# Which slot an expert's token takes: rank r in slot 7r modulo 104 instead of slot r

## The chip, the cores and the metric

One core of one Trainium2 chip runs the whole program. The metric is device time in microseconds; a comparison is made between runs of the kernel before and after on the same chip.

## The reference, cut to what matters

One decoder block over 1024 tokens of width 1024. The first two thirds (norm, projections, gated convolution, forgetting attention, merge, output projection) are not touched by the change. What matters is the mixture of experts behind it: every token chooses one group of 8 experts and in it its two best experts.

```python
lg = h @ w_rg + b_rg                     # 4 groups
g_idx = argmax(lg)
le_g = (h @ w_re + b_re) of group g_idx  # 8 experts
top_v, top_i = top_k(le_g, 2)
w_k = softmax(top_v) * p_sel
for e in range(32):
    a = silu(h @ w_gate[e]) * (h @ w_up[e])
    out = out + comb[..., e:e + 1] * (a @ w_down[e])
```

An expert's w_gate and w_up are 1024 x 256 each, its w_down 256 x 1024, all in float32: 3 MiB of weights an expert.

## The kernel before, in words

**Stages.** Activations and weights are split into a high and a low part (float32r), and a product is made of three matmuls. `start`, `attention` and `mid` come first; `out_proj` computes the residual sum, the second norm (written to the DRAM tensor `d_h2`, one row a token) and the routing, 256 tokens at a time; `moe` runs the 32 experts, in the order of `self.order` (one expert of each group in turn).

**Routing.** `route` finds each token's two experts and its rank in each of them: how many earlier tokens chose the same expert, counted with triangular matmuls. Then it builds, for 128 tokens and each of the two choices, a 0/1 matrix `lhs` with a row for each token and a column for each slot: `lhs[p, j]` is 1 where `slots[j]` equals the token's rank (L1053). `self.slots` is a constant row, filled by an iota on GpSimd in `route_consts` (L895, through the helper's L892). Matmuls of `lhs` with the token numbers and with the combine weights put them at (slot, expert) in the tables `tabi` and `tabw`. A slot that no token takes keeps the index 1024, which is out of bounds, and the weight 0. `route_index` and `scatter` write the same records to a table in DRAM, by rank, for the loop over overflow at the end (tokens of rank 104 and above, CAP = 104).

```python
for k, b in kb:
    eng = nc.vector if g == 3 else nc.gpsimd
    eng.tensor_scalar(lhs[:, b, k, :], self.slots, rk[:, b, k:k + 1], None, op0=ALU.is_equal)
```

**One expert.** `gather_rows` (L1370) fetches the expert's rows of `d_h2` into `xg`, 104 partitions x 4 KB, by an indirect DMA from GpSimd whose indices are the expert's column of `tabi`; a row whose index is out of bounds is left out. There are two `xg` buffers, so an expert's gather is issued as soon as the transposes of the expert two before have read theirs. `tokens` transposes the rows on TensorE (L1387) and splits them; `front` multiplies with gate and up (L1413, L1422 to L1424); `turned` transposes the activations; `back` multiplies with w_down (L1457 to L1459), scales on VectorE (L1460), and adds the 104 rows into the output with an indirect DMA that accumulates (L1461), with the same indices. An add waits for the fourth add before it.

**Order on TensorE.** `in_turn` fixes it: front of expert n up to its first piece, the turn of expert n - 1, the rest of the front, the transposes of expert n + 1, the back of expert n - 1.

**Weights.** They come in pieces of 512 KB (128 x 1024 float32), four for gate and up and two for down, or two pieces in one transfer of 1 MB. `plan_room` lays out the buffers: 34 pieces are loaded ahead (`raw_fill`, from L1183 on), and then a piece is loaded whenever one of the ring's 30 buffers becomes free (`piece_done`, `raw_next`; the transfers are issued at L1224 and L1249). All go through SP's queue, in order. ScalarE makes the high part of a piece (L1360) and VectorE the low part (L1361). Eight completion semaphores serve SP's transfers in turn, so a transfer is issued only when the eighth before it has landed.

Of the kernel before, what the change touches and what calls it, by code (L numbers as in the profile page):

```python
# [12 lines left out]
F32 = mybir.dt.float32  # L13
# [10 lines left out]
P = 128  # L24
# [64 lines left out]
class Builder:  # L89
# [797 lines left out]
    def route_consts(self, dp):  # L887
        nc = self.nc

        def iota(name, shape, pattern, base, mult):  # L890
            t = dp.tile(shape, F32, name=name, bufs=1)
            nc.gpsimd.iota(t, pattern=pattern, base=base, channel_multiplier=mult, allow_small_or_imprecise_dtypes=True)  # L892
            return t

        self.slots = iota("slots", [P, P], [[1, P]], 0, 0)  # L895
        self.val = dp.tile([P, TB, 2], F32, name="val", bufs=1)
        nc.gpsimd.iota(self.val[:, :, 0:1], pattern=[[0, TB], [0, 1]], base=P, channel_multiplier=-1,
                       allow_small_or_imprecise_dtypes=True)
        nc.gpsimd.iota(self.val[:, :, 1:2], pattern=[[-P, TB], [0, 1]], base=S - P, channel_multiplier=0,
                       allow_small_or_imprecise_dtypes=True)  # L900
        self.tacc = dp.tile([P, 2, NE], F32, name="tacc", bufs=1)
        nc.vector.memset(self.tacc[:, 0, :], float(S))
        nc.vector.memset(self.tacc[:, 1, :], 0.0)
        self.rev = dp.tile([P, NE], F32, name="rev", bufs=1)
        nc.gpsimd.iota(self.rev, pattern=[[-1, NE]], base=NE, channel_multiplier=0,
                       allow_small_or_imprecise_dtypes=True)
        self.tok = dp.tile([P, TB], I32, name="tok", bufs=1)
        nc.gpsimd.iota(self.tok, pattern=[[P, TB]], base=0, channel_multiplier=1)
        nc.vector.memset(self.csum, 0.0)
        ini = dp.tile([P, 96, 2], I32, name="ini", bufs=1)  # L910
        nc.gpsimd.iota(ini[:, :, 0:1].rearrange("p (a g e) o -> p a g (e o)", a=3, g=4),
                       pattern=[[0, 3], [P, 4], [0, 8]], base=S, channel_multiplier=1)
        nc.vector.memset(ini[:, :, 1:2], 0)
        self.tab_init = [nc.sync.dma_start(out=self.d_tab[:, q * 96:(q + 1) * 96, :], in_=ini) for q in range(3)]
        self.recs = []
# [615 lines left out]
```

## Time and profile before

| | us |
|---|---|
| median of three runs | 1213.91 (1209.13 to 1214.06) |
| the profiled execution | 1215.14 |
| its span, first to last instruction | 1213.4 |
| TensorE busy | 1124.9 |
| VectorE busy | 796.1 |
| ScalarE busy | 565.3 |
| GpSimd busy | 290.4 |

The span is that of one profiled execution; its own time is 1.2 us above the median of the runs. The experts run from about 850 us to the end. In the rows below PE is TensorE, PEld its weight loads, DVE VectorE, ACT ScalarE, POOL GpSimd, and SP the engine whose queue issues the weight transfers; a q behind an engine's name stands for its sequencer. "L1461" is a line of the kernel. An arrow with a name says what ended the wait.

### The profile page before, as it was taken

Reading aid. Unit: us, or ns where it says so; the run is one execution under the profiler, and the core shown is the slowest. Engines: PE = TensorE matmul, PEld = TensorE weight load, DVE = VectorE, ACT = ScalarE, POOL = GpSimd, SP = SyncE. Lnnn points to the kernel's source line nnn. Section 1 sums busy time; section 2 is a strip of 40 time slices with the busy share of each in tenths; the row PEclk is TensorE's granted clock in tenths of the full one; section 3 lists DMA queues with packets and bytes.
Section 4 is the critical chain, followed back from the end, with each engine's and each line's share of the span. In section 5 each row is a group of like instructions: output and inputs, shape, how many; then the busy total and the mean of one; then the engine's idle time right before and its main releaser. Section 6 shows DMA issues by size and latency. Waiting matters only on the chain. (4 is left out here: it accounts for less than half of the span.)

```text
span 1213.4 us, 15884 instructions
## 1 busy us (share of the span) xinstructions
PE 1124.9 (93%) x5489; PEld 894.9 (74%) x5489; DVE 796.1 (66%) x1527; ACT 565.3 (47%) x960; POOL 290.4 (24%) x280
## 2 busy tenths in 40 slices
PE   3799999999999989999999999996999997987984
PEld 3788888998898777788888888885666665655652
DVE  6855565565555665554666656787688887685863
ACT  6734544544543564323232222333666655564651
POOL 2030320330230120000000002545245434252431
PEclk8899999999999999999999999998999998998998
DMA  8514122112312424755665673347999989999961
GB/s 302 205 47 127 36 72 78 60 53 60 97 35 54 111 70 166 240 157 161 208 207 189 211 289 143 153 174 265 308 324 309 324 281 338 303 351 301 320 192 27
DMA packets 65427, 222.94 MB, mean 184 GB/s; under 512 B 11809, under 2 KB 16513, under 8 KB 56642
## 3 DMA queue, kind: packets, MB, share of 16 engines
q1 hardware_dynamic: 54370, 200.63, 49.3%
q0 software_dynamic: 9824, 17.09, 6.1%
q10 hardware_dynamic: 1152, 4.19, 0.9%
q8 instruction: 44, 0.72, 0.2%
q14 instruction: 37, 0.30, 0.1%
HBM read 201.57 MB, written 26.58 MB: 188 GB/s over the span
## 5 line engine op out<-in xcount | busy, mean ns | idle before, releaser
L1461 POOL DMA_INDIRECT out_dram<-y,tabi x32 | 85.5, 2672 | 152.6 <-DVE y L1460 133.3
L432 POOL TENSOR_SCALAR p<-p,su 128x128 f32<-128x128 f32 (+3 forms) x64 | 48.2, 759 | 234.2 <-DVE su L431 210.0
L101 ACT ACTIVATE wphi<-wpraw 128x1024 fp32r<-128x1024 f32 x42 | 44.6, 1063 | 122.9 <-DMA wpraw<-in_w_g_dram 53.2
L494 PE MATMUL gps<-hhi,wphi 128*128 128x512 f32 x256 | 101.6, 397 | 0.3 <-ACT wphi L101 0.3
L496 PE MATMUL gps<-hhi,wplo 128*128 128x512 f32 x256 | 101.3, 396 | 0.2 <-DVE wplo L102 0.2
L495 PE MATMUL gps<-hlo,wphi 128*128 128x512 f32 x256 | 101.2, 395 | 0.0
L446 DVE TENSOR_TENSOR pl<-pT,ph 128x512 fp32r<-128x512 f32 (+1 forms) x96 | 51.2, 552 | 46.7 <-ACT ph L445 46.3
L494 PE MATMUL cps<-hhi,wphi 128*128 128x512 f32 x192 | 77.1, 402 | 0.9 <-ACT v L325 0.6
L495 PE MATMUL cps<-hlo,wphi 128*128 128x512 f32 x192 | 76.3, 398 | 0.0
L188 DVE SCALAR_TENSOR_TENSOR adaw<-adaw,cb 128x1024 f32<-128x1024 f32 x32 | 39.2, 1225 | 55.2 <-DMA adaw<-in_w_ada_dram 55.2
L496 PE MATMUL cps<-hhi,wplo 128*128 128x512 f32 x192 | 74.9, 398 | 0.0
L445 ACT ACTIVATE ph<-pT 128x512 fp32r<-128x512 f32 (+1 forms) x96 | 44.4, 489 | 64.4 <-PE pT L442 58.8
L102 DVE TENSOR_TENSOR wplo<-wpraw,wphi 128x1024 fp32r<-128x1024 f32 x42 | 51.4, 1223 | 25.6 <-ACT wphi L101 25.6
L102 DVE TENSOR_TENSOR wplo<-waraw,wphi 128x768 fp32r<-128x768 f32 (+2 forms) x40 | 40.0, 1000 | 42.1 <-ACT wphi L101 41.2
L312 PE MATMUL qkvp<-wplo,hhi 128*128 128x384 f32 x192 | 65.8, 343 | 0.8 <-DVE wplo L102 0.8
L311 PE MATMUL qkvp<-wphi,hhi 128*128 128x384 f32 x192 | 65.5, 349 | 0.6 <-ACT wphi L101 0.6
L313 PE MATMUL qkvp<-wphi,hlo 128*128 128x384 f32 x192 | 65.2, 340 | 0.0
L1360 ACT ACTIVATE wphi<-H 128x1024 fp32r<-128x1024 f32 x39 | 41.1, 1060 | 40.7 <-DMA H<-in_w_gu_dram 18.3
L430 ACT ACTIVATE p<-p,m 128x128 f32<-128x128 f32 (+3 forms) x64 | 49.4, 774 | 22.8 <-DVE m L427 12.9
L1457 PE MATMUL yp<-wphi,ah 128*104 128x512 f32 x84 | 37.3, 444 | 22.1 <-DVE y L1460 14.6
L1370 POOL DMA_INDIRECT xg<-d_h,tabi x32 | 42.5, 1327 | 63.8 <-PE xT L1387 50.0
L494 PEld LDWEIGHTS gps<-hhi,wphi 128*128 128x128 f32 x256 | 48.1, 188 | 12.4 <-ACT wphi L101 0.8
(500 smaller groups left out, 3154.1 us busy)
## 6 DMA issues: line engine op xcount, KB each, us to landing
H<-in_w_gu_dram SPq DMA_DIRECT2D x24, 1024.0 KB
adaw<-in_w_ada_dram SPq DMA_DIRECT2D x32, 512.0 KB
wpraw<-in_w_g_dram SPq DMA_DIRECT2D x30, 512.0 KB
stage<-in_w_gu_dram SPq DMA_DIRECT2D x14, 1024.0 KB
wplo<-in_w_gu_dram SPq DMA_DIRECT2D x24, 512.0 KB
H<-in_w_d_dram SPq DMA_DIRECT2D x12, 1024.0 KB
wpraw<-in_w_d_dram SPq DMA_DIRECT2D x20, 512.0 KB
ld<-in_w_ada_dram SPq DMA_DIRECT2D x16, 512.0 KB
```

The source lines that it names most:

```text
L101: nc.scalar.activation(hi, raw, AF.Copy)
L102: (lo_eng or nc.vector).tensor_tensor(out=lo, in0=raw, in1=hi.bitcast(F32), op=ALU.subtract)
L311: nc.tensor.matmul(ps, hi[:, kc, sl], wh, start=(kc == 0), stop=False)
L312: nc.tensor.matmul(ps, hi[:, kc, sl], wl, start=False, stop=False)
L313: nc.tensor.matmul(ps, lo[:, kc, sl], wh, start=False, stop=(kc == KC - 1))
L430: nc.scalar.activation(pr, pr, AF.Exp, bias=m[:, b:b + 1], scale=-1.0, accum_out=su)
L432: nc.gpsimd.tensor_scalar(pr, pr, su, 1.0, op0=ALU.mult, op1=ALU.mult)
L446: nc.vector.tensor_tensor(out=pl[:, off:], in0=tp[:, off:], in1=ph[:, off:].bitcast(F32), op=ALU.subtract)
L494: nc.tensor.matmul(ps, wh, hi[:, kc, :], start=(kc == 0), stop=False)
L495: nc.tensor.matmul(ps, wh, lo[:, kc, :], start=False, stop=False)
L496: nc.tensor.matmul(ps, wl, hi[:, kc, :], start=False, stop=(kc == KC - 1))
L1461: ins = nc.gpsimd.indirect_dma_start(out=self.out, out_offset=bass.IndirectOffsetOnAxis(ap=idx, axis=0), in_=y, in_offset=None, bounds_che ...
```

## The change

The constant row `slots` holds another order of the same numbers 0 to 127. Before, slot j held j. Now slot 7a + b holds a + 15b, for a from 0 to 14 and b from 0 to 6, so that the token of rank r finds itself in slot 7r modulo 104 (ranks 0 to 103); slots 104 to 127 keep their own numbers. One iota becomes two.

```diff
-        self.slots = iota("slots", [P, P], [[1, P]], 0, 0)
+
+        self.slots = dp.tile([P, P], F32, name="slots", bufs=1)
+        nc.gpsimd.iota(self.slots[:, 0:105].rearrange("p (a b) -> p a b", b=7), pattern=[[1, 15], [15, 7]], base=0,
+                       channel_multiplier=0, allow_small_or_imprecise_dtypes=True)
+        nc.gpsimd.iota(self.slots[:, 105:P], pattern=[[1, P - 105]], base=105, channel_multiplier=0,
+                       allow_small_or_imprecise_dtypes=True)
         self.val = dp.tile([P, TB, 2], F32, name="val", bufs=1)
```

## Rows read from the trace of the kernel before

**Rows 1.** The page: the span, and busy time of each engine.

```profile
span 1213.4 us, 15884 instructions
...
PE 1124.9 (93%) x5489; PEld 894.9 (74%) x5489; DVE 796.1 (66%) x1527; ACT 565.3 (47%) x960; POOL 290.4 (24%) x280
```

**Rows 2.** Stretches: busy time of each engine, granted clock, DMA busy share, GB/s.

```profile
core 0: us, PE busy (x) PEld busy (x) DVE busy (x) ACT busy (x) POOL busy (x), PEclk, DMA share, GB/s
10.00:20.00 10.00, 5.61 (x29) 5.15 (x30) 8.85 (x35) 8.88 (x17) 2.82 (x4) 0.91 1.02 411
860.00:980.00 120.00, 118.09 (x540) 80.59 (x541) 103.50 (x112) 82.33 (x113) 56.15 (x36) 1.00 0.99 315
980.00:1180.00 200.00, 176.26 (x771) 119.67 (x769) 145.28 (x168) 110.11 (x152) 76.51 (x34) 0.94 0.91 302
```

**Rows 3.** Timeline of GpSimd, adds alone: start, length, operation, idle time before.

```profile
873.82 2.38 POOL L1461 DMA_INDIRECT out_dram<-y,tabi  x1 [0.58 <-DVE y L1460]
...
940.87 2.32 POOL L1461 DMA_INDIRECT out_dram<-y,tabi  x1 [3.46 <-DVE y L1460]
...
961.18 2.60 POOL L1461 DMA_INDIRECT out_dram<-y,tabi  x1 [4.59 <-DVE al L1443]
...
1187.94 2.32 POOL L1461 DMA_INDIRECT out_dram<-y,tabi  x1 [10.01 <-DVE y L1460]
1194.49 1.61 POOL L1461 DMA_INDIRECT out_dram<-y,tabi  x1 [4.24 <-DVE al L1443]
1198.91 1.61 POOL L1461 DMA_INDIRECT out_dram<-y,tabi  x1 [2.81 <-DVEq L1322]
```

**Rows 4.** Waits, 980 to 1200 us: waiting, released by, total us, times, longest.

```profile
ACT wphi L1360 <- DMA H<-in_w_gu_dram: 18.3, 4, 8.7
ACT row L1360 <- DMA stage<-in_w_gu_dram: 16.6, 2, 8.4
...
PE yp L1457 <- ACT xh L1389: 7.6, 1, 7.6
```

**Rows 5.** Waits of SP's queue, 860 to 1170 us, the four largest.

```profile
SPq L1249 <- DMA H<-in_w_gu_dram: 32.1, 9, 4.9
SPq L1224 <- DMA H<-in_w_gu_dram: 24.0, 7, 4.2
SPq L1224 <- DMA stage<-in_w_gu_dram: 22.4, 7, 4.4
SPq L1224 <- DMA wplo<-in_w_gu_dram: 21.7, 14, 3.4
```

**Rows 6.** The adds at 1187.94, 1194.49 and 1198.91 us, each alone: issue to landing.

```profile
DMA to landing us min/median/max: 6.9/6.9/6.9
...
DMA to landing us min/median/max: 6.1/6.1/6.1
...
DMA to landing us min/median/max: 6.0/6.0/6.0
```

**Rows 7.** The constant row's instructions: count, shortest, median, longest ns, first and last start.

```profile
L1053 POOL TENSOR_SCALAR tlhs<-slots,rk x12: 598/610/1582, 772.4 to 825.8; 128x128 bf16<-128x128 f32 x12
...
L892 POOL IOTA slots<- x1: 251/251/251, 696.2 to 696.2; 128x128 f32 x1
...
  DVE adaw L188: 227.2, 1
```

**Rows 8.** Stretch of the last add's transfers, columns as in rows 2.

```profile
1201.00:1204.50 3.50, 0.00 (x0) 0.00 (x0) 0.00 (x0) 0.00 (x0) 0.00 (x0) 0.73 0.37 53
```

**Rows 9.** Waits, 838 to 860 us, the largest of TensorE.

```profile
PE xT L1387 <- DMA xg<-d_h,tabi: 6.6, 1, 6.6
```

**Rows 10.** The page's groups of GpSimd's indirect DMAs: busy us, mean ns, idle before.

```profile
L1461 POOL DMA_INDIRECT out_dram<-y,tabi x32 | 85.5, 2672 | 152.6 <-DVE y L1460 133.3
...
L1370 POOL DMA_INDIRECT xg<-d_h,tabi x32 | 42.5, 1327 | 63.8 <-PE xT L1387 50.0
```

## The prediction

> **What bounds the kernel now.** I read the page first: TensorE is busy for 1124.9 of 1213.4 us, so time can only be won where it waits or runs slowly [rows 1]. The table of stretches shows where that is. From 860 to 980 us, in the expert stage, TensorE works 118.09 of 120 us at a granted clock of 1.00 (the 2.4 GHz level); from 980 to 1180 us it works 176.26 of 200 us, and the clock falls to 0.94 on average [rows 2]. The timeline of GpSimd gives the pace, because each expert ends in one scatter-add. The first to the eighth start at 873.82 and 940.87 us, seven periods of 9.58 us; that is TensorE's own pace. The tenth starts at 961.18 us, 1.1 us behind that pace, and the thirtieth at 1187.94 us: twenty periods of 11.34 us [rows 3]. At 9.58 us the thirtieth would start at 873.82 + 29 x 9.58 = 1151.6 us. So some 36.3 us of the expert stage are stalls. The waits say for what: ScalarE, which splits the weights, waits for weight transfers (18.3 and 16.6 us in its two largest rows), and TensorE's down products wait behind it [rows 4]. The weights' own queue, SP, does not issue ahead either: in its four largest rows alone it waits 100.2 of 310 us for an *earlier weight transfer to land* [rows 5]. A transfer has landed when the last of the 16 DMA engines is done with its part. The stage waits, then, for the slowest of them.
>
> **Why one engine may be slower than another.** In 10 to 20 us, with weights and tokens alone, the 16 engines moved 411 GB/s; from 860 to 980 us, with gathers and adds beside the weights, 315 GB/s, at the same full busy share [rows 2]. The reference's router, run on the inputs, gives 45 to 101 tokens an expert, 64 on average (2048 over 32), packed into slots 0 upwards; the other slots hold an index out of bounds and move no row. The last three adds hold 77, 63 and 45 rows, and land 6.9, 6.1 and 6.0 us after issue [rows 6]. 40% more rows take the same time: the number of rows does not set it, the fullest group does. This is what comes out if neighbouring slots go to the same engine in equal groups. I take 13 groups of 8 (104 in equal parts, at most 16); with groups of 7 the sums below shrink by an eighth and keep their sign.
>
> **The edit itself.** One iota of 0.251 us on GpSimd becomes two. Such iotas are next to free: GpSimd had been idle 227.2 us before it, at 696.2 us, and the first reader starts at 772.4 us [rows 7]. 76 us cover a second one of the same price; uncovered it would cost 0.25 us. The readers' compare has the same shape, every matmul, copy and DMA of the experts the same count and size, and the weights and indices go through the same 0/1 matrix, so they move with the rows. No expert has over 104 tokens, so the overflow loop runs zero times before and after. No wait is added.
>
> **What an engine carries, an expert.** Weights: 3 MiB over 16 engines are 48 pieces of 4 KB; at 411/16 = 25.7 GB/s a piece takes 0.159 us: 7.65 us. A gathered row is one such piece, 0.159 us. An added row has no row of its own among other traffic, so I bound it: not under a plain piece, 0.159 us; and in the tail, where nothing else runs, 0.37 of 16 engines x 3.5 us = 20.7 us for 45 rows, 0.46 us each, first-row latency included [rows 8]. If 11.34 us were all the work of a full engine, it would be (11.34 - 7.65 - 8 x 0.159)/8 = 0.30 us; that pace still had a lead to live on, so I take 0.38, between this and the tail.
> - Before, a group of 8 that is always full (slots 0 to 39 are, with 45 tokens or more): 7.65 + 8 x (0.159 + 0.38) = 11.96 us (10.2 to 12.6).
> - After, slot 7r mod 104 puts 64/13 = 4.92 rows in each group: 7.65 + 4.92 x 0.539 = 10.30 us (9.2 to 10.7).
>
> TensorE wants 9.58 us. So before, each expert loses 2.4 us of the lead that the buffers gave the weights; the first ten experts ran without stalls, so the lead is worth about 24 us. After, 31 experts lose 0.72 x 31 = 22 us: it just lasts. At the upper price they lose 1.11 x 31 = 34 us, 10 us of stall; at 0.30 us an add, none. I take 5 us.
>
> **The sum.** Stalls removed 36.3, stalls left 5: 31.3 us. The last add is on the path, since its landing ends the work: 45 rows fill groups of 8 now and of 4 after, so 4 x 0.44 us (8 rows in the 3.5 us of that window) = 1.8 us less; between 0 and 1.8, and I take it whole. The first gather holds TensorE for 6.6 us [rows 9]; three rows fewer on its fullest engine are 3 x 0.159 = 0.5 us, twice that with a weight piece between, and I count none. Together 33.1 us. The profiled execution took 1215.14 us, 1.2 above the median of 1213.91, so 1182.0 us against its own time is **1181 us** against the median. What is late next is TensorE itself, at 9.58 us an expert; its clock, lower only where it stalls, should stay at 1.00.
>
> **Rivals.**
> - *The rows are spread already.* If the group that starts a transfer moved from DMA to DMA, each engine would have 64/16 x 0.539 = 2.2 us of rows, 9.8 us in all, before the change as after. Then nothing changes: 1214 us. Against it: 9.8 us would use up 0.2 us of lead an expert and stall nowhere, while the stage falls back 36 us. For it: the tail shows groups, not which engine a group begins on. The Trainium skill speaks for this rival: its page "DMA: Bandwidth & Descriptors", section "Why a DMA increments its semaphore by 16 and not by 1", says that a GpSimd DMA whose outer size gives fewer than 16 engines takes consecutive ones from a round-robin cursor. By that rule the sum would be zero. 7%.
> - *A common limit.* If HBM, or whatever all engines share, sets the rate, moving rows between engines wins little. A third of the stalls might still go: 1202 to 1214 us. Against it stands 411 GB/s early on, against 302 to 315 in the stage [rows 2]; for it, the mean busy share of 0.99, which unequal engines should lower unless packets that share an engine are counted over each other. The same page, section "Bandwidth", says that for HBM to SBUF the HBM side binds at about 358 GB/s for a core; the 411 GB/s of this trace disagree. 8%.
> - *GpSimd becomes the bound, and it is slower.* Descriptors are made on GpSimd: 2672 + 1327 ns an expert, 4.0 of 9.58 us [rows 10]. Filled and empty slots now alternate. If that made the lists costlier, it decides from 2.4 times on (9.58 us), and makes the kernel slower from 2.8 times (11.34 us); at three times, 12.0 us, it costs some 30 x 0.66 = 20 us: 1234 us. Against it: the last add, of 45 rows, took 1.61 us, as did that of 63, and that of 77 took 2.32 [rows 3], no trend that nears a factor of 2. 3%.
>
> That the edit doesn't do what it says I rule out: the first iota writes a + 15b to slot 7a + b, and 7(a + 15b) = 7a + b modulo 104.
>
> **How the numbers follow.** My forecast has 82%. Its own bounds: no stall left, the last add and 1 us at the first gather give 1175 us; 10 us of stall and nothing at the end, 1188 us. Beyond that the lead may be worth less than I read, or part of the limit be common: up to a third of the gain left, 1203 us. The range is 1173 to 1203 us; the rest, about 2 in 10, lies with the rivals. A measurement of this kernel tells about 0.5%, 6 us, from no change. Faster: the forecast and half of the common limit, 86%. Same: the spread rows and three parts in eight of the common limit, 10%. Slower: GpSimd and what remains of it, 4%.
>
> **What would show it.** Right: adds 9.6 to 10 us apart throughout, SP's waits for landings far shorter, TensorE busy over 190 of 200 us in the stretch that was 176, more GB/s there, and the last adds' landings unequal, in the order of their rows, and shorter than 6 us. Wrong: an unchanged pace of 11.3 us, or last adds that still land in 6 us whatever their rows (then neighbours did not share an engine). If the landings shorten and the pace does not, the limit is common; if indirect DMAs on GpSimd grow past twice their time, it is the third rival.

## The result and the profile after

The kernel with the changed slots took **1195.86 us** (median of four runs, 1192.76 to 1197.02) against 1213.63 us on the same chip: a ratio of 0.9848, 95% interval 0.9825 to 0.9871, so 17.8 us faster. The forecast was 1181 us, 33 us faster, with a range from 1173 to 1203 us. The direction and the place were right; about half of the gain came. The profiled execution took 1196.05 us and its span is 1194.3 us, 19.1 us less than before [rows 1].

The page of the kernel after, span and busy times, then GpSimd's two kinds of indirect DMA (busy us, mean ns, idle before):

```profile
span 1194.3 us, 15885 instructions
...
PE 1120.5 (94%) x5489; PEld 891.4 (75%) x5489; DVE 795.8 (67%) x1527; ACT 565.4 (47%) x960; POOL 293.0 (25%) x281
...
L1466 POOL DMA_INDIRECT out_dram<-y,tabi x32 | 87.7, 2741 | 132.2 <-DVE y L1465 105.4
...
L1375 POOL DMA_INDIRECT xg<-d_h,tabi x32 | 42.3, 1321 | 65.5 <-PE xT L1392 58.9
```

The work is the same (TensorE 1120.5 us against 1124.9); GpSimd's DMAs cost what they cost before, 2741 and 1321 ns against 2672 and 1327 [rows 10]. Lines of the kernel stand five further down: the add is L1466, the gather L1375.

The timeline of GpSimd after the change, adds alone; the same adds as in [rows 3] (first, eighth, tenth, and the last three):

```profile
875.76 2.38 POOL L1466 DMA_INDIRECT out_dram<-y,tabi  x1 [0.57 <-DVE y L1465]
...
942.81 2.32 POOL L1466 DMA_INDIRECT out_dram<-y,tabi  x1 [3.46 <-DVE y L1465]
...
963.13 2.60 POOL L1466 DMA_INDIRECT out_dram<-y,tabi  x1 [4.60 <-DVE al L1448]
...
1170.15 2.32 POOL L1466 DMA_INDIRECT out_dram<-y,tabi  x1 [8.04 <-DVE y L1465]
1176.72 1.61 POOL L1466 DMA_INDIRECT out_dram<-y,tabi  x1 [4.25 <-DVE al L1448]
1181.13 1.61 POOL L1466 DMA_INDIRECT out_dram<-y,tabi  x1 [2.81 <-DVEq L1327]
```

This is where the time went. From the first add to the tenth both kernels go at the same pace: (963.13 - 875.76)/9 = 9.71 us, and (961.18 - 873.82)/9 = 9.71 us before. From the tenth to the thirtieth it was 11.34 us an expert and is (1170.15 - 963.13)/20 = **10.35 us**: twenty periods give 19.7 us back. The last two periods are 10.98 us together, before 10.97. The first add starts 1.9 us later, at 875.76 us. The last add lands sooner; the view of the line, for the three last adds, each alone:

```profile
DMA to landing us min/median/max: 6.4/6.4/6.4
...
DMA to landing us min/median/max: 5.5/5.5/5.5
...
DMA to landing us min/median/max: 4.7/4.7/4.7
```

For 77, 63 and 45 rows these were 6.9, 6.1 and 6.0 us [rows 6]; now the add of 45 rows, too, lands clearly sooner than that of 63. The sum is 1.9 - 19.7 - 1.3 = -19.1 us, the whole difference of the spans.

The stretches that follow the lead, of the kernel after (columns as in rows 2):

```profile
940.00:980.00 40.00, 40.00 (x183) 27.13 (x182) 35.56 (x39) 28.10 (x38) 17.64 (x10) 1.00 1.03 320
980.00:1020.00 40.00, 40.00 (x185) 27.27 (x184) 37.01 (x52) 26.01 (x36) 21.45 (x9) 1.00 1.03 344
1020.00:1060.00 40.00, 36.62 (x164) 24.97 (x163) 28.66 (x32) 24.48 (x35) 12.21 (x7) 0.96 1.03 348
1060.00:1100.00 40.00, 33.28 (x141) 22.32 (x140) 28.95 (x32) 20.90 (x29) 17.76 (x8) 0.91 1.02 354
```

and the same of the kernel before:

```profile
940.00:980.00 40.00, 40.00 (x186) 27.39 (x185) 35.56 (x39) 27.05 (x38) 18.30 (x10) 1.00 0.98 318
980.00:1020.00 40.00, 33.73 (x144) 22.98 (x143) 28.32 (x44) 20.61 (x29) 12.02 (x6) 0.91 0.95 304
1020.00:1060.00 40.00, 38.67 (x178) 26.37 (x177) 31.42 (x34) 23.44 (x33) 16.06 (x8) 1.00 0.97 312
1060.00:1100.00 40.00, 31.81 (x144) 21.74 (x142) 25.19 (x27) 20.47 (x28) 17.43 (x6) 0.96 0.94 332
```

More moves in the same time (344 to 354 GB/s against 304 to 332). Yet TensorE still falls short, only one stretch of 40 us later. The adds say the same, each held against the first add plus 9.58 us a period: before, the thirteenth is 2 us late, the fourteenth 11, the twenty-second 30, the thirtieth 36; after, the sixteenth is 1 us late, the seventeenth 9, the twenty-second 17 and the thirtieth 17. The lead carries three experts further, but not to the end. What SP waits for has hardly changed. Its four largest rows from 860 to 1170 us after the change, against [rows 5]:

```profile
SPq L1254 <- DMA H<-in_w_gu_dram: 28.2, 9, 4.3
SPq L1229 <- DMA H<-in_w_gu_dram: 24.2, 7, 4.4
SPq L1229 <- DMA wplo<-in_w_gu_dram: 23.6, 14, 3.4
SPq L1229 <- DMA stage<-in_w_gu_dram: 20.1, 7, 3.8
```

They add up to 96.1 us, before 100.2: all still landings of earlier weight transfers.

### The profile page after: what moved, and what is told of

Its sections match the earlier page's. It is cut to its first block, busy times and chain, and to the rows that moved or that the text cites. A ratio compares the mean times of both kernels' runs of the same rounds, so it can differ in the third digit from the quotient of the medians.

```text
span 1194.3 us, 15885 instructions
## 1 busy us (share of the span) xinstructions
PE 1120.5 (94%) x5489; PEld 891.4 (75%) x5489; DVE 795.8 (67%) x1527; ACT 565.4 (47%) x960; POOL 293.0 (25%) x281
## 5 line engine op out<-in xcount | busy, mean ns | idle before, releaser
L1466 POOL DMA_INDIRECT out_dram<-y,tabi x32 | 87.7, 2741 | 132.2 <-DVE y L1465 105.4
L430 ACT ACTIVATE p<-p,m 128x128 f32<-128x128 f32 (+3 forms) x64 | 49.4, 773 | 22.8 <-DVE m L427 12.9
L1375 POOL DMA_INDIRECT xg<-d_h,tabi x32 | 42.3, 1321 | 65.5 <-PE xT L1392 58.9
L496 PEld LDWEIGHTS gps<-hhi,wplo 128*128 128x128 f32 x256 | 48.1, 188 | 12.5 <-DVE wplo L102 0.8
L495 PEld LDWEIGHTS gps<-hlo,wphi 128*128 128x128 f32 x256 | 48.1, 188 | 11.4
```

Source lines behind the costliest of these rows:

```text
L430: nc.scalar.activation(pr, pr, AF.Exp, bias=m[:, b:b + 1], scale=-1.0, accum_out=su)
L495: nc.tensor.matmul(ps, wh, lo[:, kc, :], start=False, stop=False)
L496: nc.tensor.matmul(ps, wl, hi[:, kc, :], start=False, stop=(kc == KC - 1))
L1466: ins = nc.gpsimd.indirect_dma_start(out=self.out, out_offset=bass.IndirectOffsetOnAxis(ap=idx, axis=0), in_=y, in_offset=None, bounds_che ...
```

## The experiments

**Theory.** A weight transfer has landed when the last of 16 parts has. Rows of experts go to the engines in equal groups of neighbouring slots, and an engine's work an expert is its 7.65 us of weights plus the rows of its group. The *fullest* group therefore sets the pace, and 7r modulo 104 leaves some groups fuller than others. Counted from the router over the 32 experts, rows in the 13 groups of 8 slots:

```
before  256 256 256 256 256 245 218 150  68  51  23   8   5
after   184 183 177 171 152 140 137 165 165 165 152 132 125
```

That is 8 rows an expert in the fullest group before, 184/32 = 5.75 after, where the prediction took the mean, 4.92. **Rival.** What the change left is of another origin (a limit of all engines together, the mean load, GpSimd, buffers), and the fullest group does not matter. All kernels below change the constant row `slots`, some also `CAP`, and two leave out adds. For each, the diff against the changed kernel; the median is that of the runs beside the kernel before, which took 1214.51, 1213.75 and 1214.3 us in the three comparisons; the changed kernel itself was not timed again there.

**Sixteen groups of 7 (spread16).** 112 slots; rank r in slot 7(r mod 16) + r div 16; 109 to 140 rows a group.

```diff
-CAP = 104
+CAP = 112
...
-        nc.gpsimd.iota(self.slots[:, 0:105].rearrange("p (a b) -> p a b", b=7), pattern=[[1, 15], [15, 7]], base=0,
+        nc.gpsimd.iota(self.slots[:, 0:112].rearrange("p (a b) -> p a b", b=7), pattern=[[1, 16], [16, 7]], base=0,
...
```

> The change, with room for 112 slots in place of 104 and rank r in slot 7(r mod 16) + r div 16: if neighbouring slots go to one engine in equal groups, 112 slots are 16 groups of 7. Rows moved by the fullest group, over the 32 experts, counted from the router: before 256, after the change 184 (not the mean of 157.5 that the prediction used), here 140. Theory (the fullest engine sets the pace): from 256 rows at 1213.6 us to 184 at 1195.9 us is 0.246 us a row, so 44 rows fewer give 1185 us, or less where the weights' lead lasts, down to the stall-free 1177 us. Rival (after the change a limit common to all engines holds): the same bytes and the same 1196 us. Here also TensorE's stationary tiles and transposes are 112 columns wide in place of 104, some tenths of a us an expert at most.

Measured: **1181.46 us** (1178.19 to 1183.47), ratio 0.9724 [0.9693, 0.9755]. It is the fastest of the kernels that keep all adds, 14 us faster than the change. The stretches of this kernel from 980 us on show TensorE without gaps for three stretches and nearly so in the fourth:

```profile
980.00:1020.00 40.00, 40.00 (x185) 28.32 (x184) 36.65 (x52) 27.38 (x38) 15.73 (x9) 1.00 1.03 348
1020.00:1060.00 40.00, 40.00 (x184) 28.40 (x183) 36.04 (x39) 27.33 (x37) 18.09 (x9) 1.00 1.03 364
1060.00:1100.00 40.00, 40.00 (x184) 28.41 (x183) 32.10 (x34) 25.11 (x35) 16.51 (x8) 1.00 1.03 354
1100.00:1140.00 40.00, 38.58 (x177) 27.19 (x176) 35.44 (x39) 28.50 (x39) 26.65 (x9) 1.00 1.03 374
```

What follows: the stalls that the change left come from how the rows are spread over the engines. Nor was there a limit common to all engines at the 344 to 354 GB/s that the change moved: here they move up to 374.

**The same sixteen groups, packed (packed16).** 112 slots, slot r; six groups of 224 rows, then 209, 190, 138 and fewer.

```diff
-CAP = 104
+CAP = 112
...
-        nc.gpsimd.iota(self.slots[:, 0:105].rearrange("p (a b) -> p a b", b=7), pattern=[[1, 15], [15, 7]], base=0,
+        nc.gpsimd.iota(self.slots[:, 0:128], pattern=[[1, P]], base=0,
...
```

> Room for 112 slots, but rank r in slot r as before the change: 16 groups of 7, the fullest with 224 rows. Theory of the fullest engine: 1213.6 - 32 x 0.246 = 1206 us. Rival (alternating filled and empty slots is what helps, or the common limit): 1213 us or a little more, since nothing alternates.

Measured: 1211.48 us (1207.92 to 1214.98), ratio 0.9982 [0.9965, 1.0]. So it is not the 112 slots that make spread16 fast. But the theory wanted 1206; this is a miss, taken up below.

**Thirteen groups, even (even13).** Slot 8(r mod 13) + r div 13: the fullest group has 174 rows where the change has 184.

```diff
-        nc.gpsimd.iota(self.slots[:, 0:105].rearrange("p (a b) -> p a b", b=7), pattern=[[1, 15], [15, 7]], base=0,
+        nc.gpsimd.iota(self.slots[:, 0:104].rearrange("p (a b) -> p a b", b=8), pattern=[[1, 13], [13, 8]], base=0,
...
```

> 104 slots, rank r in slot 8(r mod 13) + r div 13, which is as even as 13 groups of 8 can be: the fullest has 174 rows, the next 168 and 166, where 7r modulo 104 gives 184, 183, 177 and 171. Theory of the fullest engine: 10 rows fewer, 2.5 us, 1193.4 us. Rival (common limit): 1196 us.

Measured: 1190.35 us (1189.15 to 1192.4), ratio 0.9812 [0.9782, 0.9841]. Pace from the tenth to the thirtieth add 10.17 us. That is below what both expected; 3.1 us of it is the first add, at 872.64 instead of 875.76 us.

**Ten of thirteen groups (spread10).** Ranks 0 to 79 over the first ten groups, the rest packed above: 214 rows in the fullest.

```diff
-        nc.gpsimd.iota(self.slots[:, 0:105].rearrange("p (a b) -> p a b", b=7), pattern=[[1, 15], [15, 7]], base=0,
+        nc.gpsimd.iota(self.slots[:, 0:80].rearrange("p (a b) -> p a b", b=8), pattern=[[1, 10], [10, 8]], base=0,
...
+        nc.gpsimd.iota(self.slots[:, 80:128], pattern=[[1, 48]], base=80,
...
```

> 104 slots, ranks 0 to 79 over the first ten groups of 8 only (slot 8(r mod 10) + r div 10), ranks from 80 packed behind: the fullest group has 214 rows. Theory of the fullest engine: 1213.6 - 42 x 0.246 = 1203.3 us. Rival (any alternation of filled and empty slots does it): 1196 us, as after the change.

Measured: 1201.28 us (1199.05 to 1205.46), ratio 0.9901 [0.9862, 0.9939]; pace 10.68 us. With these two the time goes with the fullest group, in both directions from the change.

**One full group (one_full).** Only the first group is always full, 256 rows; the other twelve have 135 to 163.

```diff
-        nc.gpsimd.iota(self.slots[:, 0:105].rearrange("p (a b) -> p a b", b=7), pattern=[[1, 15], [15, 7]], base=0,
+        nc.gpsimd.iota(self.slots[:, 0:8], pattern=[[1, 8]], base=0,
...
+        nc.gpsimd.iota(self.slots[:, 8:104].rearrange("p (a b) -> p a b", b=8), pattern=[[1, 12], [12, 8]], base=8,
...
```

> Ranks 0 to 7 in the first group of 8 slots, always full; ranks 8 to 103 spread over the other twelve groups. Rows over the 32 experts: 256 in one group, 135 to 163 in the others. Theory (the one fullest engine sets the pace, since a weight transfer has landed only when all its 16 parts have): no better than before, 1210 to 1214 us. Rival (what counts is how many engines are loaded, or the mean): one group of thirteen is a small part, so about as even13, 1190 to 1196 us.

Measured: 1206.42 us (1205.0 to 1207.67), ratio 0.9936 [0.9916, 0.9956]. It lies between, nearer the theory: one group of thirteen brings back 16 of the 23 us between even13 and the kernel before. Its stretch from 980 to 1150 us:

```profile
980.00:1150.00 170.00, 153.03 (x673) 104.28 (x672) 127.86 (x148) 98.86 (x138) 65.76 (x30) 0.94 1.00 329
```

The trace's records of semaphore increments show one engine falling behind. Below are the 16 parts of one weight transfer of each of three kernels (of 1, 0.5 and 1 MB, issued at 1094.4, 1093.5 and 1099.9 us), in us from its issue, sorted:

```
before    4.3 4.7 4.8 4.8 4.9 4.9 5.0 5.2 8.8 12.0 13.9 14.5 15.4 20.2 20.8 21.8
one_full  3.7 4.3 4.4 4.4 4.7 4.7 4.8 4.8 4.9 5.0 5.1 5.2 5.5 5.9 8.9 22.6
spread16  5.4 7.2 7.6 8.6 8.7 8.9 9.4 10.1 10.9 11.0 11.8 12.4 14.5 14.7 15.1 15.9
```

Before, half of the parts are there after 5 us and the others come up to 17 us later. With one full group exactly one part is late, and the transfer lands no sooner for it. In all 25 complete records of one_full's transfers issued between 1060 and 1124 us the last part is 9.4 to 16.2 us behind the one before it: always one part. The records do not name the engine; but eight rows cost only some 8 x 0.46 = 3.7 us by the fit below, so such a delay has piled up over several experts, on one and the same engine. And of the 16 parts of the last add, 45 rows:

```
before    2.6 2.7 2.7 2.7 2.7 2.7 2.8 2.8 2.8 2.8 5.1 5.8 5.9 5.9 6.0 6.0
after     2.6 2.7 2.7 3.9 4.1 4.2 4.2 4.2 4.3 4.3 4.5 4.5 4.5 4.5 4.6 4.7
```

Six parts with rows before (45/8 = 5.6 groups), thirteen after: the groups are 13 of 8, as taken. The Trainium skill, page "DMA: Bandwidth & Descriptors", section "Why a DMA increments its semaphore by 16 and not by 1", has the largest number up to 16 that divides the outer size, 13 for 104; these parts agree. For fewer than 16 engines the same section of the Trainium skill has consecutive engines (modulo 16) from a round-robin cursor, with the transfer's first share on the lowest-numbered of them. The cursor alone would move the full group from engine to engine, and one_full speaks against that. With the second half of the rule it fits: 13 consecutive engines leave out the lowest of all for only three of 16 starts, so, as an estimate, the first group would sit there in 13 of 16 transfers.

That the groups do move in part shows in two kernels below with nearly the same counts: spread13of16, where three of sixteen groups are almost empty, and even13, which has only thirteen groups. The parts of their weight transfers issued from 1000 to 1150 us, in us behind the first part of the same transfer, medians of the 46 and 48 complete records:

```
spread13of16  0.0 0.1 0.3 5.8 5.9 6.4 6.6 6.7 8.2 9.2 10.4 12.8 13.0 14.6 15.8 16.9
even13        0.0 0.2 2.3 3.4 3.8 4.2 4.6 5.1 5.8 6.4 7.2 7.8 8.6 10.4 11.0 12.4
```

In spread13of16 three engines stay nearly free of rows and their parts come early together. In even13 no such three stand out, so the three engines that an indirect DMA leaves out are not always the same.

**Seven of eight (packed7of8).** 13 groups of 8, nearly packed16's counts: 225 rows in six groups, 210, 191, 139.

```diff
-        nc.gpsimd.iota(self.slots[:, 0:105].rearrange("p (a b) -> p a b", b=7), pattern=[[1, 15], [15, 7]], base=0,
+        nc.gpsimd.iota(self.slots[:, 0:104].rearrange("p (a b) -> p a b", b=8)[:, :, 0:7], pattern=[[7, 13], [1, 7]], base=0,
...
+        nc.gpsimd.iota(self.slots[:, 0:104].rearrange("p (a b) -> p a b", b=8)[:, :, 7:8], pattern=[[1, 13], [0, 1]], base=91,
...
```

> 13 groups of 8, CAP 104 as before, but the first 91 ranks fill them by 7 and ranks 91 to 103 take the eighth slot of each: 225 rows in six groups, nearly the numbers of packed16 without its 112 columns. If packed16 fell short of the theory because of its 112 columns and 16 groups, this one gives what the theory gave there, 1206 us (1214 less 31/72 of the gain that 184 rows brought). If the theory itself falls short between 224 and 256 rows, it comes out as packed16, 1211 us.

Measured: 1203.38 us (1201.71 to 1204.85), ratio 0.9912 [0.9885, 0.9939], pace 10.84 us against packed16's 11.20. So the theory holds among 13 groups, and packed16 has something of its own.

**No adds, packed (noadds13_packed).** Slots as before; the scatter-adds of the first 28 experts are left out.

```diff
-        nc.gpsimd.iota(self.slots[:, 0:105].rearrange("p (a b) -> p a b", b=7), pattern=[[1, 15], [15, 7]], base=0,
+        nc.gpsimd.iota(self.slots[:, 0:128], pattern=[[1, P]], base=0,
...
+        self.backs = getattr(self, "backs", 0) + 1
+        if self.backs <= NE - 4:
+            return
         ins = nc.gpsimd.indirect_dma_start(out=self.out, out_offset=bass.IndirectOffsetOnAxis(ap=idx, axis=0),
...
```

> The order of slots as before (packed, 104 slots), with the scatter-adds of the first 28 experts left out, so that their sums are missing from the output; gathers, weights and products stay. Theory (gathers and adds of rows load the fullest engines): the fullest engine has 7.65 + 8 x 0.159 = 8.9 us an expert, under TensorE's 9.58, so no stalls: the last add starts at 1162 to 1165 us, 1178 us in all. Rival (a limit common to all engines, or stalls of another origin): 10 us of stalls or more stay, 1188 us or above.

Measured: 1180.94 us (1177.57 to 1181.67), ratio 0.972 [0.9692, 0.9749]; the last add starts at 1166.58 us. Its stretches, and then SP's three largest waits from 860 to 1170 us:

```profile
980.00:1150.00 170.00, 170.00 (x786) 116.66 (x785) 151.67 (x174) 117.69 (x161) 19.59 (x17) 1.00 0.93 314
```

```profile
SPq L1227 <- DVE mh L1364: 26.2, 9, 3.9
SPq L1252 <- DMA H<-in_w_gu_dram: 22.1, 7, 4.5
SPq L1227 <- PE aT L1441: 21.3, 9, 4.4
```

No stalls, clock 1.00, and SP now waits first for buffers to come free (VectorE's low parts, TensorE's turn): it is ahead. The gathers of the packed order alone do no harm; it takes the adds to make the stalls. It is 3 us above the theory's 1178 and 7 us under the rival's bound. The floor for any spreading of the rows is thus about 1181 us, 33 us under before.

**No adds, sixteen groups (noadds16).** spread16's slots, the same adds left out.

```diff
-CAP = 104
+CAP = 112
...
+        nc.gpsimd.iota(self.slots[:, 0:112].rearrange("p (a b) -> p a b", b=7), pattern=[[1, 16], [16, 7]], base=0,
...
+        if self.backs <= NE - 4:
+            return
...
```

> As spread16 (112 slots, sixteen groups of 7, spread), with the scatter-adds of the first 28 experts left out, so that their sums are missing. This is the floor of spread16. If 112 columns cost TensorE some 0.07 us an expert more than 104, it is 2 us behind the packed one without adds at the last add (1164 to 1167 us), and less the shorter landing about 1178 us; spread16 itself has then 3 to 4 us of stalls left. If 112 columns cost nothing, 1176 us.

Measured: 1179.16 us (1176.78 to 1180.17), ratio 0.971 [0.9683, 0.9736]; the last add starts at 1166.60 us, 0.02 us from the packed one. That the two agree is chance: the 112 columns do cost TensorE what was expected. In the timelines of GpSimd the fifth and the last gather start at 871.37 and 1130.12 us in noadds13_packed, at 869.27 and 1129.95 us here: periods of 9.58 and 9.65 us, so 0.07 us an expert, and the first seven periods of the adds are 9.65 us in each of the five kernels of 112 slots that keep all adds. The stage only begins 2.1 us sooner here, mostly because the first gather holds TensorE for 4.9 us instead of 6.8. spread16 has some 2 us of its stalls left.

**Packed from the top (packed_top, packed_top16).** Slot j holds rank 103 - j (or 111 - j of 112): the same groups on the other engines.

```diff
-        nc.gpsimd.iota(self.slots[:, 0:105].rearrange("p (a b) -> p a b", b=7), pattern=[[1, 15], [15, 7]], base=0,
+        nc.gpsimd.iota(self.slots[:, 0:104], pattern=[[-1, 104]], base=103,
...
```

> Rank r in slot 103 - r: packed as before, but from the top, so that the full groups are the last ones and the empty groups the first. Theory (the counts of the groups set the time, whichever engines they are on): 1214 us, no difference from before. Rival (the 16 engines are not alike for other reasons, and it matters which of them the full groups meet): another time by 5 us or more.

Measured: 1211.73 us (1209.99 to 1215.42), ratio 0.9983 [0.9966, 1.0]: 2.6 us under before, less than the rival's 5.

> As packed16 (112 slots, groups of 7), packed from the top: rank r in slot 111 - r. Packed from the bottom it took 1211 us, where 13 groups with the same counts took 1203. If the 16 engines are not alike and the six full groups met bad ones there, this one comes out near 1203 us; if sixteen groups cost by themselves, 1211 us again.

Measured: 1210.48 us (1207.18 to 1213.36), ratio 0.9963 [0.9944, 0.9982], as packed16. Which engines the full groups meet makes no difference that matters.

**Thirteen of sixteen groups (spread13of16).** 112 slots; ranks 0 to 90 over thirteen groups of 7, fullest 173.

```diff
-CAP = 104
+CAP = 112
...
+        nc.gpsimd.iota(self.slots[:, 0:91].rearrange("p (a b) -> p a b", b=7), pattern=[[1, 13], [13, 7]], base=0,
...
```

> 112 slots, groups of 7, but the first 91 ranks are spread over thirteen of the sixteen groups and the rest packed above: 143 to 173 rows in those, nearly the counts of even13 (165 to 174 in its fullest) without its groups of 8. If the counts set the time, 1190 us as even13; if sixteen groups cost by themselves, as packed16 against packed7of8, 1195 us or more; if the sixteen groups helped spread16 beyond its counts, 1185 us or less.

Measured: 1189.31 us (1188.1 to 1190.43), ratio 0.9794 [0.9765, 0.9823]: even13's time with even13's counts. Sixteen groups as such cost nothing that shows here.

**One full group of sixteen (one_full16).** The first group of 7 always full (224 rows), the others 105 to 136.

```diff
-CAP = 104
+CAP = 112
...
+        nc.gpsimd.iota(self.slots[:, 0:7], pattern=[[1, 7]], base=0,
...
+        nc.gpsimd.iota(self.slots[:, 7:112].rearrange("p (a b) -> p a b", b=7), pattern=[[1, 15], [15, 7]], base=7,
...
```

> 112 slots, groups of 7, the first group always full (224 rows), ranks 7 to 111 spread over the other fifteen (105 to 136). If the fullest engine alone sets the time, 1203 to 1211 us, as the two packed ones with 224 or 225 rows. If the number of loaded engines counts beside it, as one_full against before suggests (1206 against 1214), about 1196 to 1203 us; if only the mean counted, 1181 us as spread16.

Measured: 1207.68 us (1203.68 to 1209.08), ratio 0.9939 [0.9919, 0.9959]: nearly all of packed16's loss from one group of sixteen. The mean load would have given 1181.

**All of them together.** r is the rows an expert in the fullest group; the pace, in us from one add to the next, is (thirtieth add - tenth add)/20 from the profile, an average over stalls that come in steps; the last column is what a row, gathered and added, costs the fullest engine if this pace is all its work and the fullest group always falls to it, (pace - 7.65)/r:

| kernel | groups | r | pace, us | median, us | us a row |
|---|---|---|---|---|---|
| before | 13 | 8.00 | 11.34 | 1214 | 0.46 |
| packed_top | 13 | 8.00 | 11.30 | 1211.7 | 0.46 |
| one_full | 13 | 8.00 | 11.06 | 1206.4 | 0.43 |
| packed7of8 | 13 | 7.03 | 10.84 | 1203.4 | 0.45 |
| spread10 | 13 | 6.69 | 10.68 | 1201.3 | 0.45 |
| after | 13 | 5.75 | 10.35 | 1195.9 | 0.47 |
| even13 | 13 | 5.44 | 10.17 | 1190.4 | 0.46 |
| packed16 | 16 | 7.00 | 11.20 | 1211.5 | 0.51 |
| packed_top16 | 16 | 7.00 | 11.17 | 1210.5 | 0.50 |
| one_full16 | 16 | 7.00 | 11.10 | 1207.7 | 0.49 |
| spread13of16 | 16 | 5.41 | 10.23 | 1189.3 | 0.48 |
| spread16 | 16 | 4.38 | 9.83 | 1181.5 | at most 0.50 |

Among 13 groups, one price of 0.43 to 0.47 us a row gives every pace; the price is a fit, not a row of a trace. spread16's pace is near TensorE's own, 9.65 us with 112 columns, so its price is an upper bound. With sixteen groups the same rows cost 0.03 to 0.05 us more where groups are full, which is the miss of packed16 (7 x 0.05 x 20 = 7 us). Neither the engines' places (packed_top16) nor sixteen groups as such (spread13of16) account for it, and the wider columns on TensorE (noadds16) give at most 20 x 0.07 = 1.4 us of it. One candidate was not tried by a run: if thirteen groups move as estimated under one_full, and the fullest one meets the same engine in 13 of 16 transfers only, that engine is spared what it bears among sixteen. Counted so, as an estimate with 13/16 of r, the rows among 13 groups would cost 0.52 to 0.58 us, now more than the 0.48 to 0.51 among sixteen, so this alone does not make one price either. The cause stays open.

## Why the prediction was right in its direction and too high in its size

**What bounds the kernel: right.** Without adds TensorE has no gap; with one full group most of the loss is back (16 of 23 us among thirteen, 26 of 30 among sixteen). The stalls are the wait for the slowest of 16 parts. The rivals fall with the same runs. Rows that were spread already could not be won by spreading. What the prediction cited for this rival from the Trainium skill (page "DMA: Bandwidth & Descriptors", section "Why a DMA increments its semaphore by 16 and not by 1") was only half of the rule there: with the first share on the lowest-numbered engine, as given under one_full, the sum need not be zero. A common limit would not let spread16 move up to 374 GB/s where the change, still stalling, moves 344 to 354. GpSimd's descriptors cost as before.

**The edit itself: right.** The two iotas took more than thought, and are hidden; the view of the tile `slots` after the change:

```profile
L897 POOL IOTA slots<- x1: 458/458/458, 695.3 to 695.3; 128x105 f32 x1
L899 POOL IOTA slots<- x1: 157/157/157, 695.8 to 695.8; 128x23 f32 x1
...
  DVE adaw L188: 228.0, 1
```

615 ns instead of 251, behind 228 us of idle time. The first gather holds TensorE for 6.7 us, before 6.6 [rows 9]: nothing, as counted.

**What failed: "slot 7r mod 104 puts 64/13 = 4.92 rows in each group".** That is the mean. Four groups got 171 to 184 rows, up to 5.75 an expert, the others 125 to 165. By the prediction's own rule, that the slowest engine counts, the fullest group had to stand in the sum. Its formula with 5.75 is 7.65 + 5.75 x 0.539 = 10.75 us, 31 x 1.17 = 36 us less the lead of 24: 12 us of stalls, where with 4.92 it found none and took 5.

**And the lead and the price, which did not fit the kernel before.** "31 experts lose 0.72 x 31 = 22 us: it just lasts." The same formula for the kernel before gives 31 x (11.96 - 9.58) - 24 = 50 us of stalls; read were 36.3. The formula was not put to the kernel whose stalls were known. What fits all seven kernels with 13 groups but one is a smaller price over fewer experts: 1.1 us in the first ten, and behind them twenty experts at the fullest engine's 7.65 + 0.46 r. For before, packed_top, packed7of8, spread10, after and even13 this gives 36, 36, 27, 24, 15 and 13 us at the thirtieth add; measured 36.3, 35.5, 26.3, 23.2, 16.6 and 12.9. For one_full it gives 36, measured 30.6. The price is the 0.30 us an add (0.46 with the gather) that the prediction worked out "if 11.34 were all the work of a full engine" and passed over for 0.38. So the lead did not stretch to 31 experts at the smaller loss; it carried thirteen experts before (the prediction read ten) and sixteen after, so twenty experts at one pace are a fit of the totals, not of when the stalls come. Why it holds for a number of experts more than for a time was not tried by a run. SP's largest waits from 860 to 960 us, after the change, speak for buffers that limit how far the loads can run ahead:

```profile
SPq L1229 <- DVE mh L1366: 15.3, 4, 3.8
SPq L1229 <- PE aT L1443: 13.8, 5, 4.4
```

Both errors fall on one term: **"stalls left 5 us"**. Counted as in the prediction, the thirtieth add would start at 875.76 + 29 x 9.58 = 1153.6 us; it starts at 1170.15, so 16.6 us are left. That is 11.6 of the 14 us between 33.1 forecast and 19.1 measured in the spans. The later first add is 1.9 us; it starts between 870.60 and 875.76 us in the twelve kernels with all adds, in no order of their rows, and I put it down to no part of the change. The last 0.5 us is the next point.

**The last add: right, a little less.** 1.3 us instead of 1.8: four rows fewer in the fullest group, (6.0 - 4.7)/4 = 0.33 us each instead of 0.44.

**The signs.** Landings in the order of the rows, more GB/s: seen. Adds 9.6 to 10 us apart: 10.35. TensorE over 190 of 200 us in the stretch from 980 to 1180: 188.25 after the change,

```profile
980.00:1180.00 200.00, 188.25 (x841) 127.83 (x839) 159.94 (x185) 119.27 (x167) 83.06 (x37) 0.97 0.92 308
```

close, but not full, and the clock at 0.97, not 1.00. This sign was ill set: noadds13_packed, without a stall, has only 183.79 us there at 0.97, since its experts end before 1180 us. From 980 to 1150 us it has 170 of 170 us, the changed kernel 159.91. "SP's waits for landings far shorter": not seen, 96.1 against 100.2 us. It was no sign of stalls: spread16, which hardly stalls, has 99.1 us in its four largest rows from 860 to 1170 us,

```profile
SPq L1229 <- DMA stage<-in_w_gu_dram: 31.8, 8, 4.9
SPq L1229 <- DMA H<-in_w_gu_dram: 24.7, 8, 3.7
SPq L1254 <- DMA H<-in_w_gu_dram: 23.0, 8, 4.0
SPq L1229 <- DMA wplo<-in_w_gu_dram: 19.6, 15, 2.8
```

and so the like rows before [rows 5] did not show the stall either; those of ScalarE and TensorE [rows 4] did.

**Sum.** 1181 us was, without being meant so, the forecast for rows spread perfectly: the floor without adds is 1181 us, and spread16 reaches 1181.5.

## What to carry to other kernels

Where a transfer has landed only when all its parts have, count the load of the fullest engine, not the mean, and count it from the real data: with 13 engines of 16 in use and a stride of 7, the fullest carried 17% over the mean. Choose the number of slots so that it divides over all 16 engines, and deal ranks round robin over the engines' groups: that was worth 33 us here, dealing over thirteen groups 24, the stride alone 18. And a formula for the kernel after is first put to the kernel before: here it missed the stalls that the trace showed by 14 us.

## What was not expected of the hardware

Without the adds 33 us of stalls are gone, gathers and weights left as they were; by the fit among 13 groups a row costs an engine 0.30 us to add if a gathered one costs 0.159, as a 4 KB piece of weights does. And one engine of 16 that is 9 to 16 us behind costs most of what seven do: one_full takes 1206 us, even13 1190 and the kernel before 1214. Why not all of it, and why rows of full groups are dearer among sixteen than among thirteen, stays open.
